# Paged attention of eight decode sequences: cache rows of four sequences in one tile, probabilities placed by TensorE and a mask

## Chip, cores and metric

One core of a Trainium2 chip runs the whole program. The metric is device time in microseconds (us) of one execution. TensorE's clock has two levels, 1.2 and 2.4 GHz; the profile gives the granted clock as a share of 2.4 GHz.

## What is computed

One inference step of a hybrid layer: a prompt of 1040 tokens and eight decode sequences with one new token each go through a combined projection, latent attention (MLA), a recurrent branch (RWKV-7), a merge and an MLP. The change touches only the latent attention of the decode sequences, which reads 4096 past rows of each sequence from a paged cache:

```python
def softmax_merge(carry, s, vals):
    m, l, acc = carry
    m_new = jnp.maximum(m, s.max(axis=-1))
    alpha = jnp.exp(m - m_new)
    p = jnp.exp(s - m_new[..., None])
    l = l * alpha + p.sum(axis=-1)
    acc = acc * alpha[..., None] + jnp.einsum('bhqk,bkc->bhqc', p, vals)
    return (m_new, l, acc)

def page_step(carry, pages):             # over the pages of page_table
    rows = cache_kv[pages].astype(f32)   # 288 wide: 256 latent, 32 rotary
    s = jnp.einsum('bqhc,bkc->bhqk', qf, rows)
    return softmax_merge(carry, s, rows[..., :KV_LORA]), None
```

## The kernel before

The program is written as stages, and a scheduler orders each engine's instructions from the program's order and from priorities. `program` runs `decode`, a generator, beside `stage_cols`, the projections of the prompt: for each step of `cols` it takes `DN` = 2 steps of `decode`, at priority `DP`. So TensorE (PE), which takes its instructions in order, gets the attention's products in between the projections' products (`mm<-h,wh` and `mm<-h,wl`, each a 128 x 128 tile of weights against 344 or 360 columns). Each projection weight comes as `raw` from memory, is split by ScalarE (`wh`, L109) and GpSimd or VectorE (`wl`, L100), and each finished bank of `mm` is read by VectorE (`c`, L314, or `ev`, L897) or ScalarE.

`decode` treats the eight sequences in two groups of four, and each group's 4096 rows in eight blocks of 512 rows per sequence, so there are 16 blocks, numbered 0 to 15 here. For each block:

1. Four gathers (`dec_gather`, L1217), one per sequence, fetch 128 x 1152 values each into a tile `R`. There are RB = 8 such tiles, two blocks' worth, so the gather of block n+2 may start when the products of block n have read its tile. The gathers are issued by GpSimd (POOL), in POOL's order.
2. VectorE (DVE) turns each `R` in 32 x 32 squares into a tile `T` (`turned`, L1259), four instructions a block, one per sequence.
3. Scores: 36 products with the queries `qbd` as 32-column weights. The four sequences use four 32-column parts of the array and write four 32-partition parts of one PSUM tile `dc` (`dc<-T,qbd`).
4. DVE takes the maximum (`mn`, `sm`), ScalarE (ACT) the exponential of 128 columns (`Pd`, L1308).
5. DVE turns `Pd` into `Pt` (L1313), and sixteen small copies (L1318) put its squares on the diagonal of the zeroed tile `PB`: four on DVE, eight on ACT, four on POOL.
6. Values: 16 products with `PB` as weights and `R` as moving operand (`dc<-R,PB`), and DVE adds them into `acc`.

PE, DVE, ACT and POOL each run in order. The product methods all record line L92, so the trace is read by tile names.

```python
    def mm(self, out, l, r, start=True, stop=True):
        self.nc.tensor.matmul(out, l, r, start=start, stop=stop)
```

Of the kernel before, what the change touches and what calls it, by code (L numbers as in the profile page):

```python
# [35 lines left out]
KVW = 288  # L36
# [13 lines left out]
RB, DT = 8, 4  # L50
U2B, U3B, U4B, UTB, UU2 = 3, 3, 4, 2, 1
AP, MB = 2, 3
DP, DN = 300, 2
# [10 lines left out]
C_ID, C_BLK, C_RM, C_M4, C_D0, C_SEL, C_G, C_MT, C_MQ, C_S4 = 0, 128, 256, 384, 388, 772, 804, 812, 940, 1196  # L64
NCST, NC1, NC2 = 1228, 388, 812
# [6 lines left out]
class K:  # L72
# [109 lines left out]
    def consts1(self, ctx):  # L182
# [5 lines left out]
        self.d0, self.sel, self.cg = at(C_D0, 384), at(C_SEL, 32), at(C_G, 8)  # L188
# [960 lines left out]
    def dec_inputs(self, ctx):  # L1149
# [5 lines left out]
        self.dr = self.pool(ctx, "dr", RB, side="right")  # L1155
        self.dt = self.pool(ctx, "dt", DT, side="right")
# [9 lines left out]
        self.PB = dp.tile([128, 4, 4, 32], F32, name="PB")  # L1166
        nc.gpsimd.memset(self.PB, 0.0)
# [47 lines left out]
    def dec_gather(self, b, blk):  # L1215
        R = self.dr.tile([128, 4, KVW], F32, tag="R", name="R")
        self.nc.gpsimd.indirect_dma_start(  # L1217
            out=R.rearrange("p a c -> p (a c)"), out_offset=None,
            in_=self.I["cache"].rearrange("(r a) c -> r (a c)", a=4),
            in_offset=bass.IndirectOffsetOnAxis(ap=self.ix[:, b, blk:blk + 1].bitcast(U32), axis=0))  # L1220
        return R
# [20 lines left out]
    def decode(self):  # L1242
# [3 lines left out]
        todo = [(grp, blk, i) for grp in range(2) for blk in range(8) for i in range(4)]  # L1246
        Rs = {}
        at = 0

        def fetch(upto):  # L1250
            nonlocal at
            while at < min(upto, len(todo)):
                g_, k_, i_ = todo[at]
                Rs[todo[at]] = self.dec_gather(4 * g_ + i_, k_)
                at += 1

        def turned(grp, blk, i):
            T = self.dt.tile([128, 9, 4, 32], F32, tag="T", name="T")
            nc.vector.transpose(T.rearrange("p j a k -> p a j k"),  # L1259
                                Rs[grp, blk, i].rearrange("p a (j c) -> p a j c", c=32))  # L1260
            return T

        fetch(RB)
        Tn = None
        yield
        for grp in range(2):
# [8 lines left out]
            nc.vector.memset(l, 0.25)  # L1275
            acc = self.dw.tile([128, 256], F32, tag="acc", name="acc")
            ps = self.dec_tile()
            for k in range(2):
                A = self.dw.tile([128, 4, 32], F32, tag="Pd", name="A")
                nc.vector.tensor_scalar(A, self.kvs[:, k, 4 * grp:4 * grp + 4].rearrange(  # L1280
                    "p (b o) -> p b o", o=1).to_broadcast([128, 4, 32]), 0.25, None, ALU.mult)
                self.mm(ps[:, 128 * k:128 * k + 128], A.rearrange("p b o -> p (b o)"), self.ident)
            nc.vector.tensor_copy(acc, ps[:, :256])
            yield
            for blk in range(8):
                ps = self.dec_tile()
                if Tn is None:
                    Tn = []
                    for i in range(4):
                        Tn.append(turned(grp, blk, i))  # L1290
                        yield
                Tb, Tn = Tn, []
                Rb = [Rs.pop((grp, blk, i)) for i in range(4)]

                nxt = (grp, blk + 1) if blk < 7 else (grp + 1, 0)
# [11 lines left out]
                P = self.dw.tile([128, 4, 32], F32, tag="Pd", name="Pd")  # L1307
# [4 lines left out]
                Pt = self.dw.tile([128, 4, 32], F32, tag="Pt", name="Pt")  # L1312
                nc.vector.transpose(Pt.rearrange("p a k -> p (a k)"), P.rearrange("p a k -> p (a k)"))  # L1313
                for i in range(4):
# [7 lines left out]
                yield  # L1322
                for a in range(4):
                    for i in range(4):
                        self.mm(ps[32 * i:32 * i + 32, 128:384], self.PB[:, i, a, :], Rb[i][:, a, 0:256], a == 0, a == 3)
                    if nxt[0] < 2:
                        Tn.append(turned(*nxt, a))
                    if a == 1:
                        yield
                nc.vector.scalar_tensor_tensor(acc, acc, sm[:, 2:3], ps[:, 128:384], ALU.mult, ALU.add)  # L1330
                fetch(at + 4)
# [18 lines left out]
        wv = self.dr.tile([128, 4, KVW], F32, tag="R", name="R").rearrange("p a c -> p (a c)")[:, :1024].rearrange(  # L1350
# [270 lines left out]
def cst():  # L1621
# [10 lines left out]
    m[:, C_SEL:C_SEL + 32] = (i[:, None] % 8 == np.arange(32)[None] // 4) & (i[:, None] // 32 == np.arange(32)[None] % 4)  # L1632
    m[:, C_S4:C_S4 + 32] = i[:, None] % 32 == np.arange(32)[None]
    m[:, C_M4:C_M4 + 4] = i[:, None] % 64 // 16 == np.arange(4)[None]
    m[:, C_G:C_G + 8] = (i[:, None] % 4) * 8 + np.arange(8)[None]
# [117 lines left out]
```

## Time and profile before

| | |
|---|---|
| median of 3 runs | 2082.78 us (2081.57 to 2099.39) |
| the profiled execution | 2098.3 us, of which the span of instructions is 2096.5 us |
| PE busy over the span | 1945.4 us, 93% |
| stretch with the decode attention | 198 to 500 us |

Busy time is the time in which at least one instruction of an engine was running. Matmuls are pipelined, so the rate at which products follow each other is read from the difference of their starts, not from the length of one. A float32 product is recorded as two matmul instructions, so counts of `dc` are twice those of the program. The idle time before an instruction stands in brackets, with what ended it.

### The profile page before, as it was taken

To read this page: it belongs to the slowest core of one execution; us is meant where nothing else is said; L and a number is where in the kernel's file an instruction comes from. 1 tells how busy PE (TensorE), PEld (TensorE's weight loads), DVE (VectorE), ACT (ScalarE), POOL (GpSimd) and SP (SyncE) were. 2 spreads that over 40 slices of the span, in tenths; PEclk is the share of its full clock that TensorE was granted. 3 is DMA by queue.
4 is the path that set the end of the run, shared out by engine and by line. 5 is a ranking of instruction groups with operands and counts; after the bars stand their busy time and mean duration, and the time that the engine had idled before them with its cause. 6 is when DMAs were issued, how large, how long until landed. Compare 5 with 4: busy or idle time off the path is not lost.

```text
span 2096.5 us, 38743 instructions
## 1 busy us (share of the span) xinstructions
PE 1945.4 (93%) x15608; PEld 1790.6 (85%) x15608; DVE 983.0 (47%) x2009; ACT 661.2 (32%) x1509; POOL 857.1 (41%) x851
## 2 busy tenths in 40 slices
PE   8989789989989978998897899999999999999996
PEld 6988568779989866776666799999999999999996
DVE  6743535564465667777774544422212222221225
ACT  5431322212211234444445443330312213022134
POOL 3352524443322343334542433472534427153353
PEclk9999988999999977999898899999999999999998
DMA  4363454563533353332225533120201112020112
GB/s 160 131 194 143 165 182 163 190 210 105 169 102 100 106 134 84 79 88 46 76 58 133 163 135 132 41 71 26 76 21 61 46 36 72 20 71 26 56 46 81
DMA packets 169875, 209.55 MB, mean 100 GB/s; under 512 B 48256, under 2 KB 118808, under 8 KB 169568
## 3 DMA queue, kind: packets, MB, share of 16 engines
q1 hardware_dynamic: 158752, 164.75, 26.1%
q0 software_dynamic: 10944, 42.33, 6.1%
q8 instruction: 123, 2.02, 0.4%
q14 instruction: 56, 0.46, 0.1%
HBM read 158.53 MB, written 48.50 MB: 99 GB/s over the span
## 4 chain that ended last, share of the span: by engine, by line
PE 68%; DVE 13%; DMA 10%; issue 3%; POOL 2%; ACT 2%; SPq 1%; DVEq 0%; ACTq 0%; POOLq 0%
PE mm L92 41%; PE dn L92 16%; PE dc L92 4%; DVE pr L564 3%; DMA R<-cache,ix 2%; PE sv L92 2%; PE zu L92 1%; PE pv L92 1%; DVE T L566 1%; PE at L92 1%; DMA rl<-rls 1%; DVE mpart L1105 1%; DMA Ts<-T 1%; DVE x L1566 1%; POOL R L1217 1%
## 5 line engine op out<-in xcount | busy, mean ns | idle before, releaser
L92 PE MATMUL mm<-h,wh 128*128 128x344 f32 (+1 forms) x1680 | 427.3, 336 | 14.7 <-ACT wh L109 7.9
L92 PEld LDWEIGHTS mm<-h,wh 128*128 128x128 f32 x1680 | 300.1, 195 | 30.9 <-issue 8.9
L92 PE MATMUL mm<-h,wl 128*128 128x344 f32 (+1 forms) x840 | 276.4, 332 | 0.0
L100 POOL TENSOR_TENSOR wl<-raw,wh 128x512 fp32r<-128x512 f32 (+2 forms) x135 | 173.3, 1286 | 181.5 <-ACT wh L109 176.5
L92 PE MATMUL mm<-h2h,wh 128*128 128x344 f32 x768 | 246.2, 321 | 0.0
L92 PE MATMUL dn<-al,wdh 128*128 128x344 f32 (+3 forms) x768 | 246.2, 321 | 0.0
L92 PE MATMUL dn<-ah,wdl 128*128 128x344 f32 (+3 forms) x768 | 245.6, 320 | 0.0
L92 PE MATMUL dn<-ah,wdh 128*128 128x344 f32 (+3 forms) x768 | 245.2, 320 | 0.4 <-DVE x L1540 0.4
L92 PE MATMUL mm<-h2l,wh 128*128 128x344 f32 x768 | 245.0, 319 | 0.0
L92 PE MATMUL mm<-h2h,wl 128*128 128x344 f32 x768 | 241.3, 319 | 0.0
L1530 POOL TENSOR_TENSOR t<-t,r 128x344 f32<-128x344 f32 x96 | 88.7, 928 | 327.9 <-DVE t L1529 327.1
L1540 DVE TENSOR_TENSOR x<-dn,x 128x344 f32<-128x344 f32 (+3 forms) x192 | 97.9, 515 | 233.2 <-PE dn L92 233.2
L109 ACT CAST wh<-raw 128x512 fp32r<-128x512 f32 (+2 forms) x182 | 110.7, 611 | 301.7 <-PE mm L92 206.3
L92 PEld LDWEIGHTS mm<-h,wl 128*128 128x128 f32 x840 | 163.2, 195 | 3.2 <-issue 2.4
L92 PEld LDWEIGHTS dn<-ah,wdh 128*128 128x128 f32 x768 | 144.3, 188 | 0.7 <-DVE x L1540 0.7
L92 PEld LDWEIGHTS dn<-ah,wdl 128*128 128x128 f32 x768 | 144.3, 188 | 0.3
L92 PEld LDWEIGHTS mm<-h2h,wh 128*128 128x128 f32 x768 | 144.3, 188 | 0.3
L92 PEld LDWEIGHTS dn<-al,wdh 128*128 128x128 f32 x768 | 144.2, 188 | 0.3
L92 PEld LDWEIGHTS mm<-h2l,wh 128*128 128x128 f32 x768 | 144.2, 188 | 0.3
L1529 DVE TENSOR_TENSOR t<-s,mm 128x344 f32<-128x344 f32 x96 | 48.3, 510 | 203.6 <-ACT s L1527 143.6
L92 PEld LDWEIGHTS mm<-h2h,wl 128*128 128x128 f32 x768 | 143.6, 188 | 0.0
L1527 ACT ACTIVATE s<-mm 128x344 f32<-128x344 f32 x96 | 43.4, 454 | 296.2 <-PE mm L92 296.1
(398 smaller groups left out, 3918.5 us busy)
## 6 DMA issues: line engine op xcount, KB each, us to landing
raw<-w_in SPq DMA_DIRECT2D x70, 256.0 KB
raw<-w_up SPq DMA_DIRECT2D x64, 256.0 KB
raw<-w_down SPq DMA_DIRECT2D x64, 256.0 KB
z<-zs SPq DMA_DIRECT2D x8, 1280.0 KB
gts<-ev SPq DMA_DIRECT2D x48, 172.0 KB
raw<-w_o SPq DMA_DIRECT2D x22, 256.0 KB
gt<-gts SPq DMA_DIRECT2D x10, 516.0 KB
zs<-z SPq DMA_DIRECT2D x8, 524.0 KB
```

The lines of the kernel that those rows point to most:

```text
L92: self.nc.tensor.matmul(out, l, r, start=start, stop=stop)
L100: (eng or self.nc.vector).tensor_tensor(lo, src, hi.bitcast(F32), ALU.subtract)
L109: nc.scalar.copy(hi, raw)
L564: nc.vector.tensor_tensor(q, T[q_, :, 0:i + 1], Nt[q_, 0:i + 1, i].rearrange("p (o j) -> p o j", o=1).to_broadcast([q_.stop - q_.start, 8, ...
L566: nc.vector.tensor_reduce(T[q_, :, i], q, AX.X, ALU.add)
L1105: nc.vector.tensor_reduce(t[:m, j:j + 1], ps[:m, :n], AX.X, ALU.max)
L1217: self.nc.gpsimd.indirect_dma_start(out=R.rearrange("p a c -> p (a c)"), out_offset=None, in_=self.I["cache"].rearrange("(r a) c -> r (a c ...
L1527: nc.scalar.activation(s, ps, AF.Relu)
L1529: nc.vector.tensor_tensor(t, s, ps, ALU.mult)
L1530: nc.gpsimd.tensor_tensor(t, t, r2[:, ns], ALU.mult)
L1540: nc.vector.tensor_tensor(x1[:, m, n0:n0 + n], ps[:, :n], x1[:, m, n0:n0 + n], ALU.add)
L1566: eng.tensor_tensor(x1[:, k, ns], x1[:, k, ns], rs, ALU.mult)
```

## The change

One tile `R` now holds the rows of four sequences (four gathers write its four parts), in two buffers. `turned` makes two tiles for the whole block (five and four of the nine 32-wide column groups), by two DVE instructions. ACT writes the exponential four times side by side (a broadcast read), giving 128 x 512. TensorE turns each 128 x 128 part of it by a product with the identity, into a PSUM tile `pb` (also named `dc` in the trace), and one DVE product with a mask `pm` writes all of `PB`. The small copies and the turned tile `Pt` are gone. The generator has three steps a block in place of six, and `DN` is 1 in place of 2, so a block still goes with three steps of the projections. The sums of probabilities are four times as large, which `l` = 1.0 and the factor 4 in `sel` take up.

```diff
-RB, DT = 8, 4
-DP, DN = 300, 2
+DP, DN = 300, 1
...
-        self.dr = self.pool(ctx, "dr", RB, side="right")
-        self.dt = self.pool(ctx, "dt", DT, side="right")
+        self.dr = self.pool(ctx, "dr", 2, side="right")
+        self.dt = self.pool(ctx, "dt", 1, side="right")
...
+    def dec_gather(self, grp, blk):
+        R = self.dr.tile([128, 16, KVW], F32, tag="R", name="R")
+        for i in range(4):
+            self.nc.gpsimd.indirect_dma_start(
+                out=R[:, 4 * i:4 * i + 4].rearrange("p a c -> p (a c)"), out_offset=None,
+                in_=self.I["cache"].rearrange("(r a) c -> r (a c)", a=4),
+                in_offset=bass.IndirectOffsetOnAxis(ap=self.ix[:, 4 * grp + i, blk:blk + 1].bitcast(U32), axis=0))
+        return R
...
+        def turned(R):
+            T = [self.dt.tile([128, n, 16, 32], F32, tag=f"T{n}", name=f"T{n}") for n in (5, 4)]
+            for t, c0, c1 in zip(T, (0, 160), (160, 288)):
+                nc.vector.transpose(t.rearrange("p j x k -> p x j k"),
+                                    R[:, :, c0:c1].rearrange("p x (j c) -> p x j c", c=32))
             return T
...
+                R = Rn.pop(0)
                 for j in range(9):
                     for i in range(4):
                         self.mm(ps[32 * i:32 * i + 32, 0:128], self.qbd[:, j, 4 * grp + i, :],
-                                Tb[i][:, j].rearrange("p a k -> p (a k)"), j == 0, j == 8)
-                    if j % 3 == 2:
-                        yield
+                                T[j // 5][:, j % 5, 4 * i:4 * i + 4].rearrange("p a k -> p (a k)"), j == 0, j == 8)
...
-                nc.scalar.activation(P.rearrange("p a k -> p (a k)"), ps[:, 0:128], AF.Exp, bias=sm[:, 0:1], scale=SM,
-                                     accum_out=sm[:, 1:2])
+                P = self.dw.tile([128, 4, 4, 32], F32, tag="Pd", name="Pd", bufs=1)
+                nc.scalar.activation(P, ps[:, 0:128].rearrange("p (a o k) -> p a o k", o=1, k=32).to_broadcast(
+                    [128, 4, 4, 32]), AF.Exp, bias=sm[:, 0:1], scale=SM, accum_out=sm[:, 1:2])
...
-                nc.vector.transpose(Pt.rearrange("p a k -> p (a k)"), P.rearrange("p a k -> p (a k)"))
-                for i in range(4):
-                    for g in range(4):
-                        src = Pt[32 * i:32 * i + 32, :, 8 * g:8 * g + 8]
-                        dst = self.PB[32 * g:32 * g + 32, i, :, 8 * g:8 * g + 8]
-                        (nc.vector.tensor_copy, nc.scalar.copy, nc.gpsimd.tensor_copy, nc.scalar.copy)[g](dst, src)
+                pb = self.dec_tile()
+                for a in range(4):
+                    self.mm(pb[:, 128 * a:128 * a + 128],
+                            P[:, a].rearrange("p g k -> p (g k)"), self.ident)
+                PB = self.dw.tile([128, 16, 32], F32, tag="PB", name="PB", bufs=1)
+                nc.vector.tensor_tensor(PB, pb.rearrange("p (x c) -> p x c", c=32), self.pm.rearrange(
+                    "p (o c) -> p o c", o=1).to_broadcast([128, 16, 32]), ALU.mult)
...
                 yield
+                if Rn:
+                    T = turned(Rn[0])
+                yield
                 for a in range(4):
                     for i in range(4):
-                        self.mm(ps[32 * i:32 * i + 32, 128:384], self.PB[:, i, a, :], Rb[i][:, a, 0:256], a == 0, a == 3)
-                    if nxt[0] < 2:
-                        Tn.append(turned(*nxt, a))
-                    if a == 1:
-                        yield
+                        self.mm(ps[32 * i:32 * i + 32, 128:384], PB[:, 4 * a + i], R[:, 4 * i + a, 0:256], a == 0, a == 3)
                 nc.vector.scalar_tensor_tensor(acc, acc, sm[:, 2:3], ps[:, 128:384], ALU.mult, ALU.add)
-                fetch(at + 4)
+                if todo:
+                    Rn.append(fetch())
                 yield
```

The order of instructions on POOL, from the products of block 0 on, before: `R<-cache` is a gather, `PB<-Pt` a small copy, `wl<-raw` a weight's low part, `d<-c` work of the projections.

```order
L1318 COPY PB<-Pt 32x4x8 x4
L1217 DMA R<-cache,ix 128x1152 x4
L1318 COPY PB<-Pt 32x4x8 x4
L100 TENSOR_TENSOR wl<-raw,wh 128x512 x2
L302 TENSOR_TENSOR d<-c 128x1048
L1217 DMA R<-cache,ix 128x1152 x4
```

The same place on POOL with the change:

```order
L1217 DMA R<-cache,ix 128x1152 x4
L100 TENSOR_TENSOR wl<-raw,wh 128x512 x2
L302 TENSOR_TENSOR d<-c 128x1048
L1217 DMA R<-cache,ix 128x1152 x4
L100 TENSOR_TENSOR wal<-z,wah 128x1048
L100 TENSOR_TENSOR wl<-raw,wh 128x512 x2
L302 TENSOR_TENSOR d<-c 128x1048
L1217 DMA R<-cache,ix 128x1152 x12
```

The copies behind the gathers are gone, and three blocks' gathers (4, 5 and 6) stand one behind the other.

PE before, around the value products of block 1: the projection products (`mm`) are broken by single score products.

```order
L92 MATMUL mm<-h_128,wh 128x360
L92 MATMUL dc<-R,PB 32x256 x3
L92 MATMUL dc<-T,qbd 32x128
L92 MATMUL dc<-R,PB 32x256 x9
L92 MATMUL dc<-T,qbd 32x128
L92 MATMUL dc<-R,PB 32x256 x4
L92 MATMUL mm<-h_129,wh 128x360
L92 MATMUL mm<-h_128,wl 128x360
L92 MATMUL mm<-h_128,wh 128x360
L92 MATMUL mm<-h_129,wh 128x360
L92 MATMUL dc<-T,qbd 32x128
L92 MATMUL mm<-h_128,wl 128x360
```

PE with the change, from the scores of block 3 on: `dc<-cst,Pd` are the four new products with the identity.

```order
L92 MATMUL dc<-T_2459,qbd 32x128 x20
L92 MATMUL dc<-T_2460,qbd 32x128 x16
L92 MATMUL dc<-R,PB 32x256 x16
L92 MATMUL dc<-cst,Pd 128x128 x4
L92 MATMUL dc<-R,PB 32x256 x16
L92 MATMUL mm<-gh,lw1h 128x360
L92 MATMUL mm<-gh,lw1h 128x344 x2
```

The value products are those of blocks 2 and 3; 21 projection products and then the scores of block 4 follow. Scores, identity products and value products now stand in whole runs.

DVE before, from the scores to the copies of block 2: turned tiles of block 3 and the maximum of block 2 in turn.

```order
L1259 STREAM_TRANSPOSE T<-R 128x4x9x32 x2
L1304 TENSOR_REDUCE mn<-dc 128x1
L1259 STREAM_TRANSPOSE T<-R 128x4x9x32
L1305 TENSOR_TENSOR mn<-mn 128x1
L314 TENSOR_TENSOR c<-mm,rs 128x344
L1259 STREAM_TRANSPOSE T<-R 128x4x9x32
L1306 TENSOR_SCALAR sm<-mn 128x1
L1313 STREAM_TRANSPOSE Pt<-Pd 128x128
L1320 SCALAR_TENSOR_TENSOR l_2550<-l_2401,sm 128x1
L1318 COPY PB<-Pt 32x4x8 x4
```

DVE with the change, from the maximum of block 2 on:

```order
L1291 TENSOR_REDUCE mn<-dc 128x1
L1292 TENSOR_TENSOR mn<-mn 128x1
L1293 TENSOR_SCALAR sm<-mn 128x1
L1309 SCALAR_TENSOR_TENSOR l_2440<-l_2279,sm 128x1
L314 TENSOR_TENSOR c<-mm,rs 128x344
L1255 STREAM_TRANSPOSE T_2459<-R 128x16x5x32
L1255 STREAM_TRANSPOSE T_2460<-R 128x16x4x32
L1306 TENSOR_TENSOR PB<-dc,cst_120 128x512
```

The maximum is no longer split by turned tiles, but the masked product of block 2 stands behind the turned tiles of block 3; it is so in the eight even-numbered blocks.

## Rows read from the trace of the kernel before

**Rows 1.** The page: span, and part 1, PE's busy time.
```profile
span 2096.5 us, 38743 instructions
...
PE 1945.4 (93%) x15608; PEld 1790.6 (85%) x15608; DVE 983.0 (47%) x2009; ACT 661.2 (32%) x1509; POOL 857.1 (41%) x851
```

**Rows 2.** Stretches: busy us of PE, PEld, DVE, ACT, POOL; PEclk, DMA share, GB/s.
```profile
198.00:500.00 302.00, 263.73 (x2729) 221.20 (x2728) 166.48 (x343) 75.84 (x249) 129.93 (x157) 0.92 0.49 170
...
250.00:350.00 100.00, 77.27 (x689) 63.84 (x679) 50.57 (x104) 24.18 (x81) 38.29 (x51) 0.80 0.52 178
350.00:500.00 150.00, 138.76 (x1446) 117.44 (x1446) 88.58 (x185) 37.27 (x125) 68.28 (x78) 0.98 0.51 181
```

**Rows 3.** Waits of PE from 195 to 505 us: total, times, longest.
```profile
PE dc L92 <- POOL PB L1318: 19.5, 5, 5.7
PE dc L92 <- issue: 7.2, 18, 1.0
```

**Rows 4.** Timeline of POOL, 216 to 384 us: start, length, instruction.
```profile
216.40 0.98 POOL L1217 DMA_INDIRECT R<-cache,ix  x1 [3.15 <-PE dc L92]
...
221.16 0.20 POOL L1318 COPY PB<-Pt 32x32 f32<-32x32 f32 x1
227.18 0.73 POOL L1318 COPY PB<-Pt 32x32 f32<-32x32 f32 x3 [5.81 <-DMA R<-cache,ix]
...
286.65 0.96 POOL L1217 DMA_INDIRECT R<-cache,ix  x1 [6.22 <-PE dc L92]
...
299.17 0.73 POOL L1318 COPY PB<-Pt 32x32 f32<-32x32 f32 x3 [7.57 <-DMA R<-cache,ix]
...
374.11 1.00 POOL L1217 DMA_INDIRECT R<-cache,ix  x1 [4.80 <-PE mm L92]
...
383.92 0.73 POOL L1318 COPY PB<-Pt 32x32 f32<-32x32 f32 x3 [4.82 <-DMA R<-cache,ix]
```

**Rows 5.** Timeline of PE, 202 to 208 us: start, length, product, count.
```profile
202.88 0.49 PE L92 MATMUL dc<-cst,A 128*128 128x128 f32 x2
203.12 0.41 PE L92 MATMUL mm<-h,wl 128*128 128x360 f32 x1
...
206.32 0.32 PE L92 MATMUL mm<-h,wh 128*128 128x360 f32 x1
206.57 0.41 PE L92 MATMUL dc<-T,qbd 128*32 128x128 f32 x2
206.90 0.43 PE L92 MATMUL mm<-h,wh 128*128 128x360 f32 x1
...
207.34 0.48 PE L92 MATMUL mm<-h,wh 128*128 128x344 f32 x2
```

**Rows 6.** The chain that ended last: a run of projection products.
```profile
189.41 8.99 PE mm L92 x56
```

**Rows 7.** Timeline of PE: runs of score and value products, and an early identity product.
```profile
198.61 0.49 PE L92 MATMUL dc<-cst,A 128*128 128x128 f32 x2
199.03 2.17 PE L92 MATMUL dc<-T,qbd 128*32 128x128 f32 x72
...
246.62 1.82 PE L92 MATMUL dc<-T,qbd 128*32 128x128 f32 x57
...
249.41 1.72 PE L92 MATMUL dc<-R,PB 128*32 128x256 f32 x23
```

**Rows 8.** Groups of instructions of tile T: count, ns min/median/max.
```profile
L1259 DVE STREAM_TRANSPOSE T<-R x64: 1334/1378/1379, 162.4 to 474.6; 128x1152 f32<-128x1152 f32 x64
```

**Rows 9.** Groups by form, 195 to 505 us: busy, mean ns, idle before.
```profile
L314 DVE TENSOR_TENSOR c<-mm,rs 128x344 f32<-128x344 f32 x22 | 11.2, 507 | 11.3 <-PE mm L92 11.2
...
L384 ACT ACTIVATE o<-mm,hb 128x344 f32<-128x344 f32 x12 | 6.1, 545 | 3.0 <-PE mm L92 3.0
L1308 ACT ACTIVATE Pd<-dc,sm 128x128 f32<-128x128 f32 x16 | 5.9, 368 | 52.5 <-DVE sm L1306 42.9 <-DVE c L314 8.0 <-PE dc L92 1.5
...
L1304 DVE TENSOR_REDUCE mn<-dc 128x1 f32<-128x128 f32 x16 | 4.3, 271 | 10.7 <-PE mm L92 4.2 <-PE dc L92 3.7 <-remote 2.8
```

More of the change, by code (lines that the diff above doesn't have):

```diff
@@ L63 @@
 NVEC = 71
-C_ID, C_BLK, C_RM, C_M4, C_D0, C_SEL, C_G, C_MT, C_MQ, C_S4 = 0, 128, 256, 384, 388, 772, 804, 812, 940, 1196
-NCST, NC1, NC2 = 1228, 388, 812
+C_ID, C_BLK, C_RM, C_M4, C_D0, C_SEL, C_G, C_PM, C_MT, C_MQ, C_S4 = (
+    0, 128, 256, 384, 388, 772, 804, 812, 844, 972, 1228)
+NCST, NC1, NC2 = 1260, 388, 844
 class Unit:
@@ L1165, in dec_inputs @@
         nc.gpsimd.memset(self.qbd, 0.0)
-        self.PB = dp.tile([128, 4, 4, 32], F32, name="PB")
-        nc.gpsimd.memset(self.PB, 0.0)
         pt = dp.tile([128, NS], I32, name="pt")
@@ L1213, in dec_inputs @@
         self.olT = dp.tile([128, 2, 8, NS], F32, name="olT")
[L1215 to L1220, printed above, removed]
+    def dec_gather(self, grp, blk):
[5 more added lines that the diff above has]
+                in_offset=bass.IndirectOffsetOnAxis(ap=self.ix[:, 4 * grp + i, blk:blk + 1].bitcast(U32), axis=0))
         return R
@@ L1245, in decode, with fetch @@
         nc = self.nc
[L1246 to L1260, printed above, removed]
-            return T
-        fetch(RB)
-        Tn = None
+        todo = [(grp, blk) for grp in range(2) for blk in range(8)]
+        def fetch():
+            return self.dec_gather(*todo.pop(0)) if todo else None
+        def turned(R):
[3 more added lines that the diff above has]
+                                    R[:, :, c0:c1].rearrange("p x (j c) -> p x j c", c=32))
+            return T
+        Rn = [fetch(), fetch()]
+        T = turned(Rn[0])
         yield
@@ L1274, in decode @@
             nc.vector.tensor_scalar(m, ps[:, 0:1], -1.0, None, ALU.mult)
-            nc.vector.memset(l, 0.25)
+            nc.vector.memset(l, 1.0)
             acc = self.dw.tile([128, 256], F32, tag="acc", name="acc")
@@ L1278, in decode @@
             for k in range(2):
-                A = self.dw.tile([128, 4, 32], F32, tag="Pd", name="A")
+                A = self.dw.tile([128, 4, 32], F32, tag="Pd", name="A", bufs=1)
                 nc.vector.tensor_scalar(A, self.kvs[:, k, 4 * grp:4 * grp + 4].rearrange(
@@ L1286, in decode @@
                 ps = self.dec_tile()
-                if Tn is None:
-                    Tn = []
-                    for i in range(4):
-                        Tn.append(turned(grp, blk, i))
-                        yield
-                Tb, Tn = Tn, []
-                Rb = [Rs.pop((grp, blk, i)) for i in range(4)]
-                nxt = (grp, blk + 1) if blk < 7 else (grp + 1, 0)
+                R = Rn.pop(0)
                 for j in range(9):
@@ L1322, in decode @@
                 yield
+                if Rn:
+                    T = turned(Rn[0])
+                yield
                 for a in range(4):
                     for i in range(4):
-                        self.mm(ps[32 * i:32 * i + 32, 128:384], self.PB[:, i, a, :], Rb[i][:, a, 0:256], a == 0, a == 3)
-                    if nxt[0] < 2:
-                        Tn.append(turned(*nxt, a))
-                    if a == 1:
-                        yield
+                        self.mm(ps[32 * i:32 * i + 32, 128:384], PB[:, 4 * a + i], R[:, 4 * i + a, 0:256], a == 0, a == 3)
                 nc.vector.scalar_tensor_tensor(acc, acc, sm[:, 2:3], ps[:, 128:384], ALU.mult, ALU.add)
-                fetch(at + 4)
+                if todo:
+                    Rn.append(fetch())
                 yield
@@ L1349, in decode @@
         ps = self.dec_tile()
-        wv = self.dr.tile([128, 4, KVW], F32, tag="R", name="R").rearrange("p a c -> p (a c)")[:, :1024].rearrange(
+        wv = self.dr.tile([128, 16, KVW], F32, tag="R", name="R").rearrange("p a c -> p (a c)")[:, :1024].rearrange(
             "p (k v) -> p k v", k=2)
```

8 lines of the change are left out of this document (3 added, 5 removed).

## The prediction

> **What bounds the kernel now.** I read the page's busy times first. PE is busy for 1945.4 of 2096.5 us [rows 1], so a change counts only by what it does to PE: products added or removed, waits, clock, and the pace at which products follow each other. Then the table of stretches: between 198 and 500 us, where the decode attention runs, PE is busy for 263.7 of 302 us and its mean granted clock is 0.92 [rows 2]. So 38.3 us are idle there. From 250 to 350 us the clock is 0.80, which is partly the lower level of 1.2 GHz; work done at that level takes twice as long, so the loss is about busy time x (1 - clock): 77.3 x 0.20 + 138.8 x 0.02 = 18.3 us [rows 2].
>
> Third, PE's waits. The largest in the stretch is the value products waiting for POOL's small copies, 19.5 us in five pieces; 7.2 us have no releaser and lie before score products [rows 3]. POOL's timeline says why the copies are late: POOL issues four gathers, makes one copy, and starts the next only when all four gathers have landed, 5.81, 7.57 and 4.82 us later [rows 4]. Those gathers are for a later block. The copies need none of their data, but they stand behind them and wait.
>
> Last, PE's timeline, for pace. Projection products follow each other every 8.99/56 = 0.16 us [rows 6]. Where a single score product stands between them, three projections and one score take 207.34 - 206.32 = 1.02 us [rows 5]; without a break they would take 3 x 0.16 + 0.06 = 0.54 us (a score product is two passes, 57 passes in 1.82 us [rows 7]). So an excursion from 128 x 128 products to 128 x 32 ones and back costs 0.47 us, 0.235 us a change of shape. The Trainium skill, "TensorEngine Tiling (Array Packing)", Key Properties, says that changing the tiling mode drains the TensorE; this trace agrees, with that 0.47 us.
>
> **The change, part by part.** All terms are for PE, against the profiled execution of 2098.3 us (1.8 us more than its span).
>
> *Copies on POOL.* All 64 go, and with them the wait behind gathers: -19.5 us [rows 3]. Copies on ACT and DVE go too; neither engine bounds the stretch (75.8 and 166.5 us of 302 [rows 2]), so that is worth nothing by itself.
>
> *Score runs.* Score products stood between single turned tiles and were broken by them; the 7.2 us without a releaser lie there. Now a whole block is turned before its scores: -7.2 us, and what replaces it is counted below as a wait for turned tiles.
>
> *Clock.* Nearly all of the 18.3 us follows the long waits of the 250 to 350 us stretch. I expect one long wait to stay (block 4, below), so 4 us of low clock stay: -14.3 us.
>
> *Changes of shape.* Counted in the order of PE's instructions from the first scores to the last value product, changes between 32-column products and 128-column ones fall from 105 to 53, since the runs are whole: 52 x 0.235 = -12.2 us.
>
> *Products with the identity.* 16 x 4 are added. The kernel has the same product elsewhere: its two passes start at 202.88 and the next product at 203.12, 0.24 us [rows 5]; at 198.61 the product behind it changes shape and starts 0.42 us later [rows 7]. The ends are 64 x 0.24 = 15.4 and 64 x 0.42 = 26.9 us. I take 15.4, because most identity products stand among 128-column products as the first row does, and changes of shape are already counted. In 13 of the 16 places the four stand alone among projections, which is no change of shape, but of number format; between nothing and a full excursion (13 x 0.47 = 6.1 us), I take 3 us.
>
> The Trainium skill, "TensorE: Matmul & The Clock Gate", LDWEIGHTS, gives columns/1.2 ns for a load, 107 ns for 128 columns. If no load hid behind a product, an estimate by that page would be four pieces of 107 ns, 0.43 us a product and 27 us in all. The row with 0.24 us says that they do overlap, so the sum goes by the row.
>
> *Exponential and mask.* ACT writes 512 values: 0.368 us for 128 and 0.545 us for 344 [rows 9] make some 0.68 us. The mask on DVE is 0.507 us x 512/344 = 0.75 us at most [rows 9]. From the last score to the identity product that is about 0.27 + two small operations + 0.68, some 1.6 us; in the order, 13 to 49 projections (2.1 us and more) cover it everywhere but at block 3, where the 2.2 us of value products of block 2 do (32 passes at 1.72/23 = 0.07 us [rows 7]). The 0.75 us of the mask lie under projections or scores. Cost 0. If that cover failed, both would show, 16 x 0.3 + 16 x 0.75 = 17 us, but only if PE ran dry at every block.
>
> *Gathers and turning: the new waits.* The four gathers of a block take, from the first issue to the last landing, 10.8, 12.5 and 9.8 us [rows 4]; I take 11.0. Turning a block is 4 x 1.378 = 5.5 us on DVE [rows 8], now in two pieces of 3.1 and 2.4 us. Before, the first tile could be turned when one gather had landed; now it takes all four. They can start when the value products of two blocks earlier have ended.
> - Block 4: between the value products of block 2 and the scores of block 4 stand the identity products of block 3 (1.0 us), its value products (2.2) and 21 projections (3.4): 6.6 us. Needed are 11.0 + 3.1 = 14.1, so PE waits 7.5 us, and 1.1 more for the second piece.
> - Even blocks 2, 6, 10, 12, 14: their mask stands on DVE behind the turning of the next block, so from the value products of the block before to their own at least 11.0 + 5.5 + 0.75 = 17.2 us pass. PE has 63 to 71 projections (10.1 to 11.4 us), a score run (2.3), identity products (1.0), part of a score run (1.3 to 2.3) and two excursions (0.9), 16 to 17 us. A wait of 0.7 us each, 3.5 in all; 11 at the longest gather, none at the shortest.
> - The second pieces of the other blocks: some 3 us together.
>
> Together +15 us; 8 and 22 us at the shortest and longest gather. Behind DVE's wait stand reads of projection banks (L314); with four banks of about 24 x 0.16 = 3.8 us each, they hold PE only in block 4, where it waits already.
>
> *POOL.* Three blocks' gathers stand in a row, and low parts of weights behind them. Before, they stood behind copies that waited for landings; now only behind issues. I count nothing.
>
> Sum: -19.5 - 7.2 - 14.3 - 12.2 + 15.4 + 3 + 15 = -19.8 us, so 2078.5 us for the profiled execution. That execution is 15.5 us above the median of the three runs; taking the same gain off 2082.78 gives 2063.0 us.
>
> **The rivals.**
>
> *Gathers hidden.* Waits at the shortest gather (8 us), no low clock left, nothing for the change of format: -19.5 - 7.2 - 18.3 - 12.2 + 15.4 + 8 = -33.8, 2049 us. For it: gathers as short as 9.8 us occur [rows 4], and POOL and ACT are freer. Against it: block 4 has only 6.6 us of cover.
>
> *Given back on PE.* Identity products at 0.42 us (26.9), format at 6.1, the longest gathers (22), 10 us of low clock left: -19.5 - 7.2 - 8.3 - 12.2 + 26.9 + 6.1 + 22 = +7.8, 2091 us. For it: the 12.5 us gather [rows 4], and 0.42 us where the shape changes [rows 7]. Against it: changes of shape would be counted twice.
>
> *Slower: the whole-tile wait.* With one tile for four sequences every piece of turning needs the last of four gathers, and in even blocks the mask stands behind it. Each microsecond beyond 11 then costs one in each of six blocks (2, 4, 6, 10, 12, 14). At 16 us that is 30 us, and each such wait would bring about 2.5 us of low clock, 15 us: -19.8 + 45 = +25, 2108 us. It decides from about 15.5 us of gather. For it: DMA is the engine under the stretch's waits and the weights share its queues. Against it: the rows show 9.8 to 12.5 us under the same load [rows 4].
>
> **How the numbers follow.** The forecast has 0.53 (2063; alone 2052 to 2076), hidden gathers 0.22 (2049), given back 0.15 (2091), slower 0.10 (2108). A measurement of this kernel tells about 1% from no change, so the bounds are 2062 and 2104. The forecast lies almost on the lower one: 0.24 of it below and 0.29 above. Faster is 0.24 + 0.22 = 0.46, the same 0.29 + 0.15 = 0.44, slower 0.10. The range goes from 2045, just below hidden gathers, to 2088, just short of the given-back end, and leaves out about 2 in 10.
>
> **What would show it right or wrong.** In the changed profile no wait of PE names POOL's `PB`; the largest in the stretch is that of the scores of block 4 for a turned tile, 6 to 9 us; four identity products take 1.0 us; the clock from 250 to 350 us is above 0.9 but for one drop; gathers still land in 10 to 12 us. I am wrong if identity products take 1.7 us a block, if waits for turned tiles come at most blocks, if the exponential or the mask holds PE, or if the stages behind 500 us move by more than 5 us in length, since I count nothing there.

## The result and the profile after

The changed kernel takes 2056.7 us (median of 4 runs, 2054.7 to 2058.7) against 2082.2 us before on the same chip (2080.5 to 2099.4): ratio 0.9856, 95% interval 0.981 to 0.990, a gain of 25.5 us. Two later measurements, each on another chip, gave 0.9843 (0.9799 to 0.9888) and 0.9832 (0.9792 to 0.9871). The forecast was 2063.0 us, with a range from 2045 to 2088, and faster as the likeliest of the three outcomes, so it was right in direction and 6.3 us too high; how much of that nearness is luck stands below. The profiled execution took 2057.6 us.

The page of the changed kernel, span and part 1 (before: [rows 1]):

```profile
span 2055.7 us, 38608 instructions
...
PE 1925.1 (94%) x15736; PEld 1785.2 (87%) x15736; DVE 975.4 (47%) x1913; ACT 639.8 (31%) x1381; POOL 838.7 (41%) x786
```

Its stretches, with the columns of [rows 2]: length, busy us of PE, PEld, DVE, ACT and POOL, PEclk, DMA share, GB/s.

```profile
198.00:500.00 302.00, 276.32 (x2920) 248.39 (x2920) 181.71 (x278) 61.41 (x136) 126.01 (x101) 0.96 0.53 183
250.00:350.00 100.00, 89.79 (x989) 81.53 (x993) 61.07 (x92) 19.43 (x47) 39.52 (x32) 0.95 0.57 195
350.00:500.00 150.00, 140.61 (x1401) 127.50 (x1394) 91.85 (x144) 28.64 (x64) 59.57 (x47) 0.96 0.51 179
```

PE has 12.6 us more busy time in the 302 us, and from 250 to 350 us the granted clock is 0.95 where it was 0.80. By the rule of the prediction (busy time x (1 - clock)) the two later stretches lose 89.79 x 0.05 + 140.61 x 0.04 = 10.1 us to the clock instead of 18.3.

PE's waits from 195 to 505 us in the changed kernel (before: [rows 3]):

```profile
PE dc L92 <- DVE T L1255: 5.7, 8, 1.3
PE mm L92 <- DVE c L314: 5.6, 3, 2.2
PE mm L92 <- ACT g L373: 4.9, 2, 3.7
PE dc L92 <- ACT Pd L1296: 3.8, 2, 2.4
PE dc L92 <- DVE PB L1306: 3.7, 3, 1.6
```

POOL's `PB` and the waits without a releaser are gone. What is new is small and spread: turned tiles `T`, the exponential `Pd`, the mask product `PB`.

A ledger of the whole span shows where the time came from. In the windows view I cut each span into pieces of 5 us and took from each PE's idle time and busy time x (1 - granted clock); what is left is PE's work at full clock.

| us | idle | lost to the clock | work | span |
|---|---|---|---|---|
| before | 151.1 | 67.0 | 1878.4 | 2096.5 |
| changed | 130.6 | 60.9 | 1864.2 | 2055.7 |
| difference | -20.5 | -6.1 | -14.2 | -40.8 |

The difference is larger than 25.5 us because the profiled execution of before lies 15 us over its median. Of the idle time, 14.7 us went between 190 and 550 us (40.4 to 25.7); of the clock's loss, 7.7 us (19.0 to 11.3). The work fell although 64 products were added, which by themselves cost 14 to 17 us (below), so 28 to 31 us of other work went. Fewer changes of shape account for some 17 us of that; the rest is not traced to anything.

### The profile page after: what moved, and what is told of

Same layout as the page of the kernel before. It is cut to its first block, busy times and chain, and to the rows that moved or that the text cites. A ratio compares the mean times of both kernels' runs of the same rounds, so it can differ in the third digit from the quotient of the medians.

```text
span 2055.7 us, 38608 instructions
## 1 busy us (share of the span) xinstructions
PE 1925.1 (94%) x15736; PEld 1785.2 (87%) x15736; DVE 975.4 (47%) x1913; ACT 639.8 (31%) x1381; POOL 838.7 (41%) x786
## 4 chain that ended last, share of the span: by engine, by line
PE 56%; DVE 10%; DMA 5%; POOL 2%; issue 2%; ACT 1%; SPq 1%; DVEq 0%; POOLq 0%; ACTq 0%
PE mm L92 31%; PE dn L92 17%; DVE pr L564 2%; PE sv L92 2%; PE pv L92 2%; PE at L92 2%; PE zu L92 1%; DVE T L566 1%; PE mx L92 1%; DVE mpart L1105 1%; DVE x L1555 1%; DMA Nt<-Ns 1%; PE sc L92 1%; DMA Ns<-Sm 1%; DMA qkst<-qr 0%
```

## The experiments

All kernels below were timed beside the kernel before on one chip; a gain or a loss is the distance of the medians of that series unless a ratio is named. The first series takes the two halves of the change apart, the second asks why they need each other, the third tests the answer.

### The kernel before, unchanged, on the chip of the first series

> The kernel before, unchanged, for a profile of an execution near its median (2082 us; the profile shown was 16 us above). Theory (the copies on POOL behind the gathers cost 19.5 us of waits and most of 18 us of low clock): PE waits of 15 to 22 us for POOL's PB between 195 and 505 us here too, and the 16 us lie mostly in other stages. Rival (the waits were those of a slow execution): under 10 us of them here.

The profiled execution took 2093.9 us (median of before in this series 2089.7). Its wait for POOL's `PB` and its stretch from 250 to 350 us:

```profile
PE dc L92 <- POOL PB L1318: 21.2, 6, 5.7
250.00:350.00 100.00, 77.20 (x737) 63.64 (x738) 52.23 (x109) 24.49 (x79) 37.10 (x49) 0.85 0.53 180
```

The wait is as in [rows 3], so in this the profile that the prediction rests on is a typical one. The low clock there is not quite: 0.85 against 0.80, and from 190 to 550 us the clock's loss by the ledger is 13.8 us against 19.0.

### No copies on POOL (small tiles)

```diff
-   (nc.vector.tensor_copy, nc.scalar.copy, nc.gpsimd.tensor_copy, nc.scalar.copy)[g](dst, src)
+   (nc.vector.tensor_copy, nc.scalar.copy, nc.vector.tensor_copy, nc.scalar.copy)[g](dst, src)
```

> Before, with the four POOL copies of each block given to DVE; nothing else changed by hand, but the scheduler's order has 117 changes of array shape in place of 105. Theory: the waits for POOL go (-19.5), most of the low clock goes (-14), shape changes +12 x 0.235 = +3: about 2082 - 30 = 2052 us. Rival (the wait for a gather is hidden there and comes back at the next turned tile, and what the change gains comes from whole runs): 2072 us or more.

Measured: 2083.7 us (10 runs, 2077.1 to 2095.5), ratio 0.9973 (0.995 to 0.9996): 6 us, where the theory wanted 2052. A miss: the time is on the rival's side of 2072. The rival's reason is not borne out, though, since waits for turned tiles are 3.2 us here and whole runs by themselves gain nothing (the big tiles alone, below). PE's waits for POOL's copies are gone from the profile, but in the median most of their worth does not arrive. The last series comes back to this.

### The identity products and the mask alone (small tiles)

```diff
-   Pt = ...; nc.vector.transpose(Pt, P); 16 copies to self.PB
+   pb = self.dec_tile()
+   for a in range(4):
+       self.mm(pb[:, 128 * a:128 * a + 128], P[:, a]..., self.ident)
+   nc.vector.tensor_tensor(PB, pb..., self.pm..., ALU.mult)
```

> Before, with its gathers and turned tiles of one sequence, but with the identity products and the mask of the change. 87 changes of shape. Theory: -19.5 -14 +15.4 +3 -18 x 0.235 = -19, about 2063 us. Rival (whole runs make the gain): 2075 us or more, since score products still stand singly.

Measured: 2074.7 us, ratio 0.9919 (0.9895 to 0.9943), 15 us less than before. This is at the rival's bound of 2075 rather than at 2063. PE's idle time without a releaser before decode products is 13.8 us in 31 pieces: the score runs are still cut by single tiles.

### The big tiles alone (copies as before, POOL's among them)

```diff
-   pb = self.dec_tile(); four identity products; PB = pb x mask
+   nc.vector.transpose(Pt, P)
+   for i in range(4):
+       for g in range(4):
+           (nc.vector.tensor_copy, nc.scalar.copy, nc.gpsimd.tensor_copy, nc.scalar.copy)[g](dst, src)
```

> The change's tiles of four sequences and whole runs of scores, but with the old turned tile Pt and the sixteen copies, four of a block on POOL. 99 changes of shape. Theory: POOL's copies stand behind gathers again, so PE waits of 15 us or more for PB, less 15.4 + 3 for the identity products: about 2080 us. Rival: whole runs make the gain, and without identity products it is faster than the change, 2045 us or less.

Measured: 2092.2 us, ratio 1.0026 (1.0005 to 1.0047). Neither my 2080 nor the rival: half of the change gives nothing at all. Its waits of PE, 195 to 505 us, say why:

```profile
PE dc L92 <- POOL PB L1308: 17.5, 8, 4.1
PE dc L92 <- DVE T L1257: 8.0, 4, 3.5
```

POOL's `PB` is back, and the waits for turned tiles come on top.

### The second series: the changed kernel again

> The changed kernel itself, on the chip of the three kernels beside it. Theory (the gain has three parts that need one another: 15 us less waiting, 8 us of granted clock, the rest fewer changes of the products' shape): ratio to before 0.984 to 0.990, with PE's waits of the decode stretch led by turned tiles (4 to 8 us) and no POOL copy named. Rival (the first measurement fell on a good chip): ratio above 0.991.

Measured: 2057.3 us, ratio 0.9843. Waits for turned tiles are 1.5 us here, under the 4 to 8 I expected, and 5.0 us in the third series: this term scatters from execution to execution.

### Identity products issued twice

```diff
+   for _ in range(2):
        self.mm(pb[:, 128 * a:128 * a + 128], P[:, a]..., self.ident)
```

> The changed kernel with each of the 64 identity products issued twice. Theory (one costs 0.24 us, as the products with the identity in the trace): 64 x 0.24 = 15 us above the changed kernel, and all of it in the time. Rival 1 (loading a fresh tile of 128 columns decides: 0.42 to 0.43 us each): 27 us above. Rival 2 (the identity products lie in PE's waits for exponential and mask anyway, so that they are free): under 5 us above.

Measured: 2067.9 us, ratio 0.9906 (0.9869 to 0.9943), 10.6 us above the changed kernel beside it, 0.17 us for each of 64. The intervals leave some 12 us of doubt on the difference, so that rival 1 is out and the theory (15) and rival 2 (under 5) are both near; the ledger is sharper, with 16.8 us more work (1864.2 to 1881.0), 0.26 us each. Sharper still are the starts on PE's timeline: at full clock four identity products take 0.81 us from their first start to that of a projection behind them, and eight take 1.70, so one more takes 0.22. So they cost PE about what the row of before said. Whether a part of that fills time in which PE would have waited stays open: the idle time is 125.0 us, against 130.6 in the first execution of the changed kernel but 124.7 in the one beside it.

### Big tiles, 16 copies, none on POOL

```diff
-   (nc.vector.tensor_copy, nc.scalar.copy, nc.gpsimd.tensor_copy, nc.scalar.copy)[g](dst, src)
+   (nc.vector.tensor_copy, nc.scalar.copy, nc.vector.tensor_copy, nc.scalar.copy)[g](dst, src)
```

This edit is made on the version with big tiles and copies.

> The changed kernel's gathers, big tiles and whole score runs, but with the probabilities transposed on VectorE and placed by 16 copies on VectorE and ScalarE (none on POOL). Theory (big tiles gave nothing with the copies because POOL's copies, 17.5 us of PE's waits, stayed): without them half of the way from the version with POOL copies (ratio 1.003) to the changed kernel or more: ratio 0.987 to 0.995, PE's waits for PB under 6 us. Rival (16 copies cost by themselves, wherever they run, and only TensorE and a mask set the run of scores free): ratio 0.997 or more, and waits for PB of DVE and ACT of 8 us and more in place of POOL's.

Measured: 2048.9 us, ratio 0.9812 (0.9768 to 0.9856), more than the theory asked for. Moving 64 copies of 0.2 us from POOL to VectorE is worth 2 per cent here (1.0026 to 0.9812), some 45 us (0.0214 x 2087). So TensorE and the mask are not needed for a gain of this size. Not all of it lies where the copies ran: a table at the end of the experiments puts 25 us into the decode stage and 18 us behind it. PE's waits for `PB` are 5.3 us, all for ScalarE's copies.

### Scores in four steps again

```diff
-DP, DN = 300, 1
+DP, DN = 300, 2
...
+   if j % 3 == 2:
+       yield
```

> The changed kernel with its scores issued in four steps (a break behind every third of the nine column groups) and steps twice as close: the score products are again cut by projections. Theory (the changes of shape are worth about as much as they were found to cost in the kernel before, 0.35 us for one visit of projections among scores): the number of visits decides; as the order shows 55 changes of shape again, nearly the same as in the changed kernel, the time stays within 4 us of it. Rival (whole score runs count by themselves, for instance through the clock or because the steps of the RWKV work move with them): 8 us or more above the changed kernel.

Measured: 2063.1 us (2051.3 to 2068.5), ratio 0.9861 (0.9807 to 0.9915). It lies 5.8 us above the changed kernel, between the theory's 4 and the rival's 8, and the intervals overlap: undecided.

### Why the copies wait

In the version with big tiles and POOL copies, this is the timeline of POOL, DVE and ACT at one block:

```profile
271.97 0.94 POOL L1219 DMA_INDIRECT R<-cache,ix  x1 [0.30 <-issue]
276.29 0.78 DVE L1308 COPY PB<-Pt 32x32 f32<-32x32 f32 x4
276.32 0.21 POOL L1308 COPY PB<-Pt 32x32 f32<-32x32 f32 x1 [3.41 <-DMA R<-cache,ix]
277.16 1.88 ACT L1308 COPY PB<-Pt 32x32 f32<-32x32 f32 x8
279.11 5.04 DVE L1257 STREAM_TRANSPOSE T<-R 128x2560 f32<-128x2560 f32 x2 [0.78 <-DMA R<-cache,ix]
279.14 0.73 POOL L1308 COPY PB<-Pt 32x32 f32<-32x32 f32 x3 [2.61 <-DMA R<-cache,ix]
```

POOL's last gather is issued at 272.91 and its first copy runs at 276.32, 0.03 us behind DVE's first: the gathers, still under way, do not hold it. (Its bracket names a gather, but in the built program this copy waits for no gather.) The other three run at 279.14, within 0.03 us of the turning, which waits for the gathers' landing. So it isn't POOL's line that holds them. In [rows 4] the same can be seen: one copy, then 5 to 8 us, then three. The order of POOL in the built kernel before, with the semaphores that an instruction waits for, has it in writing (block 1, small tiles; the first number is the place in POOL's order, and DMASW are the gathers' semaphores):

```
82 L1217 DMA R<-cache,ix 128x1152 [waits PE_49,Pool_49]
83 L1217 DMA R<-cache,ix 128x1152 [waits PE_49] x3
84 L1318 COPY PB<-Pt 32x4x8 [waits DVE_49]
85 L1318 COPY PB<-Pt 32x4x8 [waits DMASW3_49,DMASW4_49,DMASW2_49,DMASW1_49]
86 L1318 COPY PB<-Pt 32x4x8 x2
```

In 14 of the 16 blocks the second copy waits for four gathers whose data it does not read. In the built programs this wait stands at POOL copies whose source begins at partition 32 or above (sequences 1 to 3 of a block), and at none that begins at partition 0 (sequence 0); once one copy has waited, the next ones need not. The third series uses that: POOL gets the four copies of sequence 0, and VectorE and ScalarE the others, so that the counts stay 4, 4 and 8.

### POOL's copies from partition 0 only, big tiles

```diff
-   (nc.vector.tensor_copy, nc.scalar.copy, nc.gpsimd.tensor_copy, nc.scalar.copy)[g](dst, src)
+   (nc.gpsimd.tensor_copy if i == 0 else nc.vector.tensor_copy if g == i else
+    nc.scalar.copy if g else nc.vector.tensor_copy if i == 3 else nc.scalar.copy)(dst, src)
```

> Big tiles with the 16 copies a block, four of them still on POOL (64 in all, as in the version at ratio 1.003), but POOL has the four of the first sequence (source partitions 0 to 31) in place of one of each sequence. In the built program a POOL copy whose source begins at partition 32 or above carries a wait on the four gathers in flight; those from partition 0 carry none. Theory (that wait on the gathers is what the POOL copies cost): time near the version without any POOL copy, ratio 0.977 to 0.990, PE's waits for POOL's PB under 5 us. Rival (the copies cost because they stand in POOL's line among the gathers' issues, 4 x 1.25 us, and behind other work there): still 0.995 or more, with waits for POOL's PB of 10 us and more.

Measured: 2059.1 us against 2094.1, ratio 0.9838 (0.9801 to 0.9875), from 1.0026. The theory holds, though the version without POOL copies stays about 10 us below. PE's waits in it:

```profile
PE dc L92 <- DVE T L1257: 4.5, 6, 1.1
PE dc L92 <- POOL PB L1308: 3.7, 2, 3.3
```

### The same edit alone in the kernel before

> The kernel before with only this edit: POOL has the four copies of the first sequence of a block in place of one of each sequence (ScalarE 8, VectorE 4, POOL 4, as before). Theory (the wait on the gathers in flight): at least what moving all POOL copies to VectorE gave, ratio 0.990 to 0.998, PE's waits for POOL's PB from about 20 us to under 5. Rival (POOL's line): ratio 0.999 or more, those waits over 10 us.

Measured: 2059.7 us against 2094.1, ratio 0.9847 (0.9809 to 0.9884). This one line, with small tiles, cut score runs and no mask, gives what the whole change gives (0.9832 beside it). It leaves the copies on the same three engines in the same numbers; the scheduler's order changes a little with it (97 changes of shape for 105). First the order of POOL at the place shown above:

```
83 L1217 DMA R<-cache,ix 128x1152 [waits PE_49] x4
84 L1318 COPY PB<-Pt 32x4x8 [waits DVE_49,Pool_49]
85 L1318 COPY PB<-Pt 32x4x8 [waits Pool_49] x3
```

Then POOL's waits in the kernel before from 190 to 505 us (first fence), and POOL's timeline in the edited one (second):

```profile
POOL PB L1318 <- DMA R<-cache,ix: 36.4, 8, 7.6
POOL wl L100 <- ACT wh L109: 30.9, 13, 10.2
```

```profile
243.90 0.98 POOL L1217 DMA_INDIRECT R<-cache,ix  x1
...
247.87 0.94 POOL L1217 DMA_INDIRECT R<-cache,ix  x1 [0.30 <-issue]
248.82 1.92 POOL L1318 COPY PB<-Pt 32x32 f32<-32x32 f32 x4
```

The 36.4 us of POOL's waiting for gathers are gone; four copies start 0.01 us behind the issue of the fourth gather. PE's waits for POOL's `PB` fall from 19.5 to 1.1 us:

```profile
PE dc L92 <- issue: 7.4, 20, 1.0
PE dc L92 <- POOL PB L1318: 1.1, 2, 0.7
```

By the ledger of the whole span idle time falls by 23.8 us (151.1 to 127.3), the clock's loss by 6.1 (67.0 to 60.9), the work by 4.8. In the decode attention alone, from the first score product to the last value product, the same products take 262.2 us in place of 291.3. Length, busy us of PE, PEld, DVE, ACT and POOL, PEclk, DMA share and GB/s, before and then with the edit:

```profile
199.00:490.30 291.30, 253.03 (x2654) 211.07 (x2653) 163.48 (x337) 73.30 (x244) 125.32 (x155) 0.92 0.50 172
```

```profile
196.90:459.10 262.20, 239.04 (x2653) 197.30 (x2653) 167.52 (x335) 73.64 (x244) 128.25 (x155) 0.97 0.55 191
```

Idle time falls from 38.3 to 23.2 us there, and the loss to the clock (busy time x (1 - clock)) from 20.2 to 7.2, some 13 us.

What stays open in part is why moving all POOL copies to VectorE gave only 6 us with small tiles. Its profiled span is 2076.4 us and its idle time between 190 and 550 us is low (26.7 us), so the waits at the copies did go. Its decode stage ends 16.8 us earlier than that of the unchanged kernel on the same chip (562.5 and 579.3 us, first start of tile `pr`, which belongs to the next stage), that of the one-line version 25.8 us earlier (553.5). The order of PE has 117 changes of shape there against 97 in the one-line version, 20 x 0.235 = 4.7 us, about half of those 9 us. Behind the stage neither gains more than 5 us on the unchanged kernel. That names no cause for the rest, and its ten runs lie mostly above its profile.

### The best version and the changed kernel, side by side

> The version with big tiles and the 16 copies on VectorE and ScalarE once more (the same text as the one at ratio 0.9812). Theory (it saves the 64 identity products, some 10 us as the doubled ones showed, and pays some 4 us for more changes of shape): 4 to 10 us under the changed kernel, ratio 0.978 to 0.984. Rival (its 8 us were scatter): within 3 us of the changed kernel.

> The changed kernel once more, to stand beside the others on one chip. Both theories: ratio 0.983 to 0.989.

Measured: 2048.5 us (2046.1 to 2056.9), ratio 0.98 (0.9764 to 0.9836), for big tiles with copies on VectorE and ScalarE; 2060.4 us (2046.6 to 2063.7), ratio 0.9832 (0.9792 to 0.9871), for the changed kernel. With the second series it is below the changed kernel twice, by 8.4 and 11.8 us, though the intervals overlap. I expected the gain inside the decode stretch, from the identity products. The windows up to 550 us and from there to 1360 us (length, PE busy, PEclk, DMA share, GB/s) put it elsewhere; the changed kernel first, then the best version:

```profile
0.00:550.00 550.00, 508.64 (x4413) 0.97 0.52 174
550.00:1360.00 810.00, 737.85 (x7029) 0.93 0.35 97
```

```profile
0.00:550.00 550.00, 508.84 (x4254) 0.97 0.50 173
550.00:1360.00 810.00, 747.01 (x7123) 0.94 0.36 100
```

Up to 550 us both are busy alike. Behind it the best version has 9.2 us less idle time. Which waits of the later stages those are, and why the order of the decode decides it, was not followed further.

The first start of tile `pr` divides each profiled execution into the part that ends with the decode stage and the rest of the span (us):

| | to `pr` | from `pr` |
|---|---|---|
| before; again | 584.6; 579.3 | 1511.9; 1512.8 |
| small tiles, no copies on POOL | 562.5 | 1513.9 |
| small tiles, POOL's copies from partition 0 | 553.5 | 1508.3 |
| small tiles, identity products and mask | 571.1 | 1509.2 |
| big tiles, copies as before | 581.4 | 1509.0 |
| big tiles, POOL's copies from partition 0 | 550.3 | 1511.3 |
| big tiles, no copies on POOL; again | 556.2; 552.7 | 1491.1; 1493.0 |
| changed; second; third series | 547.9; 546.2; 547.2 | 1507.8; 1508.2; 1511.2 |

Wherever POOL's copies no longer wait for gathers, the decode stage ends 8 to 38 us earlier than in the kernel before. Up to there the changed kernel is ahead of every other version in the table; the best one overtakes it only in stages that none of the edits touch.

## Why the prediction was right

The sum was -19.8 us for a measured -25.5 by the medians. Between the profiled executions, from which its terms were read, 40.7 us lie (2098.3 to 2057.6). Step by step:

- *Copies on POOL (-19.5) and the clock (-14.3).* This step carries the result. Without the wait on gathers, and with nothing else changed by hand, the kernel before gains 1.5 per cent, 32 us (24 to 40 by its interval), for the 33.8 us of the two terms together. In the decode attention itself these are 15.1 us of idle time and some 13 us of clock. The place was right, and the reason was wrong in one point: the prediction said that the copies "stand behind" the gathers in POOL's line. They do, but that costs only the issue. What holds them is a wait that the program carries, and the two versions with 64 POOL copies from partition 0 show it: the copies still follow gathers and no longer wait. The clue was in [rows 4]: the first copy of a block ran, and only the next three were late. In the changed kernel the clock's part was somewhat smaller than stated: 8.2 us by the rows shown above, 12.4 us in the execution of the third series (0.95 in 250 to 350 us, 0.99 behind it), and less again if the other execution of before is the measure, which loses 15.7 us by the same rule where the prediction's lost 18.3.
- *Score runs (-7.2).* Not settled. No wait without a releaser is named in the changed profile above, but 3.4 us in the third series and 4.8 in the second, and the second execution of before has 5.0 us of them, not 7.2. The gain lies between nothing and all of it.
- *Changes of shape (-12.2).* Under-sized. I took from PE's timeline, wherever no wait stands, the time by which a product follows one of another kind later than by the pace of its kind (0.16 us a projection, 0.0285 a score pass, 0.066 a value pass). An excursion to a lone score product costs 0.48 us at the median of 24 places before, as the prediction had it: the product starts 0.09 us late, the projection behind it starts 0.28 us later than two passes take in a run, and the projection after that 0.11 us late. An excursion to a whole run of 72 passes costs 0.25 us (3 places after): 0.09, 0.05 and 0.11. The step back to a projection is the same in both, 0.20 us behind the last pass; what costs more is the lone product, whose second pass follows the first by 0.13 us. Summed over the stretch, all changes together make some 17 us less after than before, an estimate by these paces. So a price read from lone products does not carry over to whole runs. The Trainium skill, "TensorEngine Tiling (Array Packing)", Key Properties, has a change of mode drain the TensorE but gives no price; the trace agrees that it costs.
- *Identity products (+15.4).* Right as work (16.8 us for 64 more by the ledger, 14 by the starts); as time 10.6 us, with some 12 us of doubt. Four take 0.81 us from their first start to that of a projection behind them and 0.98 to that of a score product, for the 1.0 written. The estimate from the Trainium skill, "TensorE: Matmul & The Clock Gate", LDWEIGHTS (27 us in all if no load is hidden), is out by this run.
- *Number format (+3).* Not seen. Identity products start 0.16 us behind a projection, as another projection would, and a projection behind them starts 0.03 us after their last pass, not late. 3 us too much.
- *Exponential and mask (0).* Their lengths were right, the cover was not complete. The groups of tiles `Pd`, `PB` and `T` in the changed kernel (count, ns min/median/max, first and last start, form):

```profile
L1296 ACT ACTIVATE Pd<-dc,sm x16: 669/687/689, 202.1 to 457.5; 128x512 f32<-128x512 f32 x16
...
L1306 DVE TENSOR_TENSOR PB<-dc,cst x16: 646/688/692, 205.4 to 463.3; 128x512 f32<-128x512 f32 x16
...
L1255 DVE STREAM_TRANSPOSE T<-R x30: 2262/2560/2846, 193.6 to 448.8; 128x2560 f32<-128x2560 f32 x15, 128x2048 f32<-128x2048 f32 x15
```

  0.69 us each for 0.68 and at most 0.75 expected, and 2.85 + 2.26 = 5.1 us for turning a block, where 5.5 was taken. PE still waits 7.5 us for the two (3.8 + 3.7), some 4 in the other executions. The prediction named this among the signs that it is wrong, and the sign came.
- *Waits for gathers and turning (+15).* Too high: turned tiles cost 5.7 us here, 1.5 and 5.0 in the other two executions, and with `Pd` and `PB` the new waits are 13.2, 5.0 and 8.9 us. The place of block 4 was worked out rightly and named wrongly. From the end of block 2's value products (240.8) to block 4's scores (254.4) 13.6 us pass; the prediction had 11.0 + 3.1 = 14.1. But PE's idle time in between falls on whoever comes last at each step:

```profile
242.12 1.16 PE L92 MATMUL dc<-cst,Pd 128*128 128x128 f32 x8 [1.37 <-ACT Pd L1296]
244.91 3.37 PE L92 MATMUL dc<-R,PB 128*32 128x256 f32 x32 [1.63 <-DVE PB L1306]
...
250.06 0.43 PE L92 MATMUL mm<-gl,lw1h 128*128 128x360 f32 x1 [0.93 <-DVE gl L100]
...
254.38 1.30 PE L92 MATMUL dc<-T,qbd 128*32 128x128 f32 x40 [1.31 <-DVE T L1255]
256.48 1.08 PE L92 MATMUL dc<-T,qbd 128*32 128x128 f32 x32 [0.80 <-DVE T L1255]
```

  Together 6.0 us for the predicted 8.6, and only 2.1 of them name `T`, so no single wait of 6 to 9 us appears. The value products of block 3 also take 3.37 us for 2.2: from 244.9 to 248.3 us the granted clock was 0.56, close to the lower level of 1.2 GHz, after PE had stood idle for 2.75 of the 4 us from 241 to 245. That stretches the cover.
- *Stages behind 500 us (nothing).* From the first start of tile `pr` to that of `dn` 823.0 us pass before (584.6 to 1407.6) and 818.8 after (547.9 to 1366.7): 4.2 us, under the bound of 5.

So the direction rests on the first step, which the runs confirm. That the forecast came within 6.3 us is in part luck. The changed kernel gained 25.5, 29.7 and 33.7 us by the medians of three series, and 40.7 us between the profiled executions, so the sum was 6 to 21 us short. Most errors point the same way: the changes of shape were worth more, and the number format and the new waits cost less, by a few microseconds each; the clock and perhaps the score runs, taken a few too good, made up for part of it. Of the rivals, hidden gathers (2049) came closest after the forecast: its 8 us of waits fit the second series (5.0), but low clock was left, which it had at nothing. The slower one did not come: gathers still land in 10.3 us at block 4 (issue at 241.12, turning at 251.39). Its argument that the weights share the gathers' queues is not borne out by the profile of before: from 195 to 505 us it has two large queues, and one of them carries the gathers alone (8064 packets, 144 for each of 56).

The experiments also correct the reading of the change as a whole. Its big tiles are worth nothing as long as POOL's copies wait (1.0026); its mask, which takes the copies off POOL, is worth 15 us alone; and one line in the kernel before does as much as all of it.

## What to carry to other kernels

When one of several like instructions on an engine runs on time and the next ones are late, ask what differs between them, and look at what each waits for in the built program before blaming the line they stand in: here it was the partition at which the source begins. Before redesigning the data's path around a wait, try the edit that removes only the wait; it tells what the rest of the design has to earn by itself. A wait removed in a long stretch can bring back more than its length, since the clock follows it: in the decode attention 15.1 us less idle time and some 13 us less loss to the clock for a wait of 19.5 us. And ask at which mark in the span a gain has arrived: the best version here wins in stages that were not edited.

## What the runs showed that was not expected

- Waits on gathers in flight stand, in the built programs of this case, on POOL copies whose source begins at partition 32 or above. They cost 36.4 us of POOL and 19.5 us of PE before, and 1.5 per cent of the time. In every version here partition 0 is also sequence 0, so the two are not told apart. Why the program is built so, and whether the chip needs it, was not tried.
- 64 copies of 0.2 us each (13 us of work, spread over 16 blocks) are worth some 45 us when they are moved from POOL to VectorE in the version with big tiles, 25 of them in the decode stage, and some 40 us, 31 of them in the decode stage, when POOL keeps 64 copies but from partition 0.
- The second pass of a score product alone between projections starts 0.13 us behind the first; in a run passes follow each other every 0.0285 us. The projection behind starts 0.20 us after the last pass either way.
- An identity product added to PE's work costs 0.22 us between starts at full clock, and 0.26 us of work by the ledger.
